# A two-layer trunk: seven, then eight column groups over the first k tiles in four phases, larger modulation loads, mixer A begun in the last phase

## The chip, the cores and the metric

The kernel runs on one core of a Trainium2 chip. The metric is the device time of one execution in microseconds (us). In this text PE is TensorE (matmuls), PEld its weight loads, DVE is VectorE, ACT is ScalarE, POOL is GpSimd, and SP is the engine whose queue issues most DMAs. Numbers such as L319 are lines of the kernel before; where a line of the changed kernel is meant, that is said.

## The reference

Two layers work on 384 tokens of width 2048, 128 of a context and 256 latents. What matters here is layer 0 and its order:

```python
sh, sc, gt = split(silu(cond) @ w_mod + b_mod, 3)          # w_mod [2048, 6144], two conditions
h = rmsnorm(x) * (1 + sc) + sh
aq, af_f, af_b, ai, ag, bq, bk, bv, bg = split(h @ w_in)   # w_in [2048, 7680]
o_a = hgrn2(silu(aq), gates(af_f), gates(af_b), ai)        # mixer A, 8 heads, both directions
o_b = attention(bq, bk, bv)                                # mixer B
y = x + gt * (concat(gated o_a, gated o_b) @ w_out)        # w_out [2048, 2048]
```

Layer 1 has a modulation, an input product, an attention and an output product of its own. Each product is made in three terms, high by high, high by low and low by high, of values that are split into a high and a low part.

## The kernel before, in words

**The products.** The k dimension of 2048 is 16 tiles of 128. A trunk product is made in column groups of 512 columns, a group in pieces of two k tiles: `w_piece` (L312) loads 512 KB of weights on SP's queue into one of four buffers `raw`, ACT writes the high part `whi` (L317, three buffers) and DVE the low part `wlo` (L319, two buffers). A piece is 24 matmuls of 384 columns, or 18 of 512 when the tokens are on the partitions. The sums of a group stand in four PSUM buffers `mm` (`psm`, L57), four or three to a group.

**The start.** Layer 0's input needs shift and scale of a k tile before that tile can enter a product. So the start goes through the k tiles in five phases, `START` = (0, 1), (1, 3), (3, 6), (6, 10), (10, 16). In each, `start_group` (L652) makes the partial product of six column groups (`first`: the forget gates `lf` and queries `qs` of mixer A) over the phase's k tiles and adds it to a tile in SBUF: a copy on ACT in the first phase, an addition on DVE (L670) later. Between the pieces `start_mod` (L672) loads the shift and scale weights of the next phase's k tiles, 512 KB at a time, into the same four buffers `raw`, and multiplies them on PE (L683, L691), after which `modulate` makes that part of the input.

**The background.** Everything else of the modulations is made on DVE, 1024 columns at a time, by `mod_acc` (L223): for each of 16 k tiles a load of 512 KB into one of two buffers `mraw`, and two additions to `acc` (L235), one for each condition. The list is, in order, layer 1's scale and shift (four parts), then the gates of layer 0, columns 0 to 1023 (`mod_gates`, L260, which ends with matmuls that spread `acc` over the partitions, L277 and L278, and additions to the tiles `tK` and `tL`, L279). After each piece of a product `pump` (L297) adds a rate to a counter and runs one unit (one k tile) of the list for each whole number in it. A step of a mixer takes a quarter of its own weight from that counter. `finish` (L303) runs units until a named gate is there.

**The order after the start.** Mixer A (`hgrn_prep`, `hgrn_heads`) is queued and takes a step after each piece of five groups: two for its values `vt`, two for the queries of mixer B, one for its keys and values. Then come four gate groups, with mixer B, and the output product. Its first group ends with `finish((0, 0))`, and its three sums are multiplied with the gate in `tK` (L991), which frees its PSUM buffers. The gates of columns 1024 to 2047 enter the list there. A scheduler places the instructions of each engine in one fixed order; an engine runs them in that order.

Of the kernel before, what the change touches and what calls it, by code (L numbers as in the profile page):

```python
# [14 lines left out]
P = 128  # L15
# [7 lines left out]
RATE0 = 0.6  # L23
# [7 lines left out]
SRAW = 3  # L31
# [5 lines left out]
START = ((0, 1), (1, 3), (3, 6), (6, 10), (10, 16))  # L37

# columns of the constant table
# [5 lines left out]
def trunk_kernel(ctx: ExitStack, tc: tile.TileContext, I, O):  # L45
# [8 lines left out]
    # what only the start needs  # L54
# [20 lines left out]
    # The mixers are traced step by step, one step after each piece of a trunk product, so that TensorE  # L75
    # has trunk products to run while a mixer's data is on its way through the other engines.
# [35 lines left out]
    # x, token-major: block 0 is the context, blocks 1 and 2 the latents  # L112
# [9 lines left out]
    # rows of parameters, turned into columns; the conditions first  # L122
# [17 lines left out]
    # silu of the two conditions, columns (k tile, condition)  # L140
# [18 lines left out]
    def load_params():  # L159
# [3 lines left out]
        # lower bound of the forget gates: softmax over the depth axis, first entry  # L163
# [38 lines left out]
    # ---------------------------------------------------------------- modulation  # L202
# [6 lines left out]
    def mod_cols(l, k0, nk, cp):  # L209
        # columns k0.. of the modulation, from sums [128, nk, 2] or [128, 2, 2, 2]  # L210
# [12 lines left out]
    def mod_acc(l, c0):  # L223
        # 1024 columns on VectorE, summed over the k tiles
# [15 lines left out]
    def mod_part(l, k0):  # L240
        # shift or scale of 8 k tiles, as columns
# [18 lines left out]
    def mod_gates(l, g0, tags, ready):  # L260
        # two times 512 columns of the gate as rows on all partitions, [128, 2, 512]
# [21 lines left out]
    # modulations in the background, pace[1] steps after each piece of a trunk product; gates that have  # L283
    # a place to go to come before the columns of layer 1
# [37 lines left out]
    def group(w, c0, hq, fm, after=None, n=512):  # L322
        # n columns of a product: 4 tiles [128 features, 384 tokens], or 3 tiles [128 tokens, n features]
# [33 lines left out]
    # ---------------------------------------------------------------- norm and modulation of x  # L357
# [5 lines left out]
    def turn_x(x, xt, copy):  # L363
        # [128 tokens, 512] x 3 -> [128 features, 4, 384]; copy(out, in, k tile of x)
# [6 lines left out]
    def rpow(out, ss, n, eps):  # L371
        # (ss / n + eps) ** -0.5
# [3 lines left out]
    def rstd_row(ss):  # L376
        # the norm's factors of all tokens, on all partitions
# [13 lines left out]
    def modulate(l, q, xt, rb, hq=None, parts=((0, 4),)):  # L391
        # x of a quarter, [128 features, 4, 384], normed, modulated in place and split
# [13 lines left out]
    def modulate_scaled(l, q, xt, rb, parts):  # L406
        # the same for x that the scale is in already
# [14 lines left out]
    def split(dst, k, src, scale=None):  # L422
        # dst = (high, low) tiles of a quarter, src [128, 384] in SBUF or PSUM, times a column
# [47 lines left out]
    def rope(x, nh, cw, sw):  # L471
        # in place on x [128, nh*128]
# [199 lines left out]
    def start_mod(k0, k1):  # L672
        # shift and scale of a few k tiles on TensorE, four k tiles of the product side by side
        for k, nk in pairs(k0, k1):
            n, k8 = nk * P, 8 // nk
            ps = px()
            for part in range(2):
                for i in range(2 * nk):
# [6 lines left out]
                    if part == 0 or i < 2 * nk - 1:  # L685
                        yield
# [21 lines left out]
    for i, (k0, k1) in enumerate(phases):  # L708
# [13 lines left out]
        if i == 1:  # L722
            load_params()
# [422 lines left out]
```

## Time and profile before

| | us |
|---|---|
| device time, three runs | 1397.18, 1395.74, 1390.61 |
| median | 1395.74 |
| span of the profiled execution, first to last instruction | 1388.5 |
| PE busy, share of the span | 1346.3, 97% |
| DVE busy | 1022.3, 74% |
| ACT busy | 651.8, 47% |
| DMA moved | 265.45 MB, mean 191 GB/s |

The profile gives the profiled execution's span; its time with what lies around the span is not listed by itself, and the median of the runs is 7.2 us above the span. A busy share of PE is an upper bound, since the end of a matmul is modelled. The page cuts the span in 40 slices; other views group instructions by line, list waits by who waited for whom, follow the chain of work that ended last, or give busy times of chosen stretches.

### The profile page before, as it was taken

The page shows a single profiled execution, that of the slowest core. Times are in us where ns is not written, and L with a number is a line of the kernel's source. Part 1 is how long each engine was busy: PE and PEld are TensorE (multiplying, and loading weights), DVE is VectorE, ACT ScalarE, POOL GpSimd, SP SyncE. Part 2 cuts the span into 40 slices and gives each one's busy share as a digit, 9 for nine tenths or more (in the row PEclk, how much of TensorE's full clock was granted, in tenths as well). Part 3 has the DMA queues.
Part 4 walks back from the last instruction along what each step waited for, and adds up shares of the span by engine and source line. Part 5 has one row for each costly group of instructions (what it writes and reads, how often), then busy time and mean ns, then how long its engine had stood idle before and what let it go on. Part 6 is the DMA issues. An engine that isn't in the chain of part 4 may idle for free.

```text
span 1388.5 us, 19820 instructions
## 1 busy us (share of the span) xinstructions
PE 1346.3 (97%) x7435; PEld 1152.5 (83%) x7435; DVE 1022.3 (74%) x1605; ACT 651.8 (47%) x1302; POOL 79.1 (6%) x86
## 2 busy tenths in 40 slices
PE   6999999999999999999998998999999999999998
PEld 5677888997888877788977896878888899997788
DVE  6587657998996989994896358985656664488753
ACT  4422333485654535655532345434866763352221
POOL 1000000000000032101000000100000001000000
PEclk9999999999999999999999998999999999999999
DMA  9999988647554576665477543774323345457742
GB/s 280 310 319 304 305 289 299 222 125 238 171 172 133 150 219 199 199 213 182 152 235 250 167 148 89 232 246 143 105 79 90 95 113 173 131 174 226 238 162 71
DMA packets 142239, 265.45 MB, mean 191 GB/s; under 512 B 8960, under 2 KB 54976, under 8 KB 142144
## 3 DMA queue, kind: packets, MB, share of 16 engines
q1 hardware_dynamic: 136288, 245.73, 56.2%
q0 software_dynamic: 5600, 18.39, 4.3%
q8 instruction: 58, 0.95, 0.3%
q14 instruction: 37, 0.30, 0.1%
q10 hardware_dynamic: 256, 0.08, 0.0%
HBM read 256.04 MB, written 8.13 MB: 190 GB/s over the span
## 4 chain that ended last, share of the span: by engine, by line
PE 82%; DVE 8%; DMA 5%; issue 2%; POOL 1%; ACT 1%; SPq 0%; DVEq 0%; POOLq 0%; ACTq 0%
PE mm L340 54%; PE mm L662 5%; PE mm L664 5%; PE mm L663 5%; DMA mraw<-in_l_w_mod_dram 4%; DVE acc L235 3%; PE px L520 3%; PE px L683 2%; DVE wlo L319 2%; PE px L580 1%; PE px L597 1%; POOL sm L374 1%; PE px L543 1%; PE px L368 1%; PE px L831 1%
## 5 line engine op out<-in xcount | busy, mean ns | idle before, releaser
L317 ACT CAST whi<-raw 128x1024 fp32r<-128x1024 f32 (+1 forms) x270 | 278.2, 1031 | 524.0 <-PE mm L340 392.4
L319 DVE TENSOR_TENSOR wlo<-raw,whi 128x1024 fp32r<-128x1024 f32 (+1 forms) x270 | 322.7, 1196 | 182.3 <-PE mm L340 155.0
L340 PE MATMUL mm<-wlo,hh 128*128 128x512 f32 (+1 forms) x1104 | 413.8, 375 | 13.3 <-DVE wlo L319 13.2
L340 PE MATMUL mm<-whi,hh 128*128 128x512 f32 (+1 forms) x1104 | 417.5, 378 | 1.2 <-ACT hh L417 0.8
L340 PE MATMUL mm<-whi,hl 128*128 128x512 f32 (+1 forms) x1104 | 411.7, 373 | 0.0
L235 DVE SCALAR_TENSOR_TENSOR acc<-mraw,csil,acc 128x1024 f32<-128x1024 f32 x240 | 300.9, 1278 | 37.2 <-DMA mraw<-in_l_w_mod_dram 36.9
L340 PEld LDWEIGHTS mm<-wlo,hh 128*128 128x128 f32 x1104 | 209.6, 190 | 53.3 <-DVE wlo L319 19.5
L340 PEld LDWEIGHTS mm<-whi,hh 128*128 128x128 f32 x1104 | 209.2, 190 | 39.2 <-issue 1.7
L340 PEld LDWEIGHTS mm<-whi,hl 128*128 128x128 f32 x1104 | 209.2, 190 | 35.9
L662 PE MATMUL mm<-hh,whi 128*128 128x384 f32 x384 | 134.1, 354 | 4.5 <-ACT whi L317 2.1
L340 PE MATMUL mm<-hh,whi 128*128 128x384 f32 x384 | 131.4, 342 | 0.8 <-DVE tM L613 0.8
L663 PE MATMUL mm<-hl,whi 128*128 128x384 f32 x384 | 130.6, 340 | 0.4 <-DVE hl L403 0.4
L340 PE MATMUL mm<-hh,wlo 128*128 128x384 f32 x384 | 129.4, 337 | 0.0
L340 PE MATMUL mm<-hl,whi 128*128 128x384 f32 x384 | 129.0, 336 | 0.0
L664 PE MATMUL mm<-hh,wlo 128*128 128x384 f32 x384 | 121.8, 340 | 0.1
L662 PEld LDWEIGHTS mm<-hh,whi 128*128 128x128 f32 x384 | 73.2, 192 | 21.1 <-issue 12.2
L664 PEld LDWEIGHTS mm<-hh,wlo 128*128 128x128 f32 x384 | 71.8, 189 | 4.1 <-DVE wlo L319 2.3
L663 PEld LDWEIGHTS mm<-hl,whi 128*128 128x128 f32 x384 | 73.3, 191 | 1.7 <-issue 1.0
L340 PEld LDWEIGHTS mm<-hh,whi 128*128 128x128 f32 x384 | 72.2, 188 | 2.8 <-DVE tM L613 1.6
L340 PEld LDWEIGHTS mm<-hl,whi 128*128 128x128 f32 x384 | 72.2, 188 | 0.9
L340 PEld LDWEIGHTS mm<-hh,wlo 128*128 128x128 f32 x384 | 72.1, 188 | 0.7 <-issue 0.2
L555 ACT ACTIVATE p<-px,nb,rs 128x384 f32<-128x384 f32 (+1 forms) x72 | 42.4, 594 | 12.2 <-DVE nb L553 8.2
(444 smaller groups left out, 1416.6 us busy)
## 6 DMA issues: line engine op xcount, KB each, us to landing
raw<-in_l_w_in_dram SPq DMA_DIRECT2D x194, 512.0 KB, 3.9
mraw<-in_l_w_mod_dram SPq DMA_DIRECT2D x192, 512.0 KB, 4.8
raw<-in_l_w_out_dram SPq DMA_DIRECT2D x64, 512.0 KB, 4.1
raw<-in_l_w_in_dram SPq DMA_DIRECT2D x12, 256.0 KB, 6.6
tK<-in_l_b_mod_dram POOLq DMA_DIRECT2D x6, 256.0 KB, 5.4
y1d<-tA POOLq DMA_DIRECT2D x2, 768.0 KB, 5.9
tD<-y1d POOLq DMA_DIRECT2D x2, 768.0 KB, 6.8
tL<-y1d POOLq DMA_DIRECT2D x2, 768.0 KB, 7.0
```

Of the source, the lines that this page charges most:

```text
L235: nc.vector.scalar_tensor_tensor(out=acc[:, c], in0=raw, scalar=s, in1=acc[:, c], op0=ALU.mult, op1=ALU.add)
L317: nc.scalar.copy(hi, raw)
L319: nc.vector.tensor_tensor(out=lo, in0=raw, in1=hi.bitcast(F32), op=ALU.subtract)
L340: nc.tensor.matmul(ps[c], lhsT=a, rhs=b, start=(kt + k == 0 and i == 0), stop=(kt + k == KT - 1 and i == 2))
L368: nc.tensor.transpose(ps[:, b * P:b * P + P], x[:, b, k * P:k * P + P], ident)
L374: nc.gpsimd.tensor_tensor(out=out, in0=out, in1=nhalf[:, 0:out.shape[1]], op=ALU.pow)
L520: nc.tensor.matmul(out, lhsT=a, rhs=b, start=(i == 0), stop=(i == len(ops) - 1))
L555: nc.scalar.activation(p[:, j], ss[j], AF.Exp, bias=nb[:, j:j + 1], scale=rs[:, i + j:i + j + 1], accum_out=sm[:, j:j + 1])
L662: nc.tensor.matmul(ps[c][:, 0:T], lhsT=wh, rhs=hh[:, kq], start=(kt + k == k0), stop=False)
L663: nc.tensor.matmul(ps[c][:, 0:T], lhsT=wh, rhs=hl[:, kq], start=False, stop=False)
L664: nc.tensor.matmul(ps[c][:, 0:T], lhsT=wl, rhs=hh[:, kq], start=False, stop=(kt + k == k1 - 1))
L683: nc.tensor.matmul(ps[32 * (j % 4):32 * (j % 4) + 32, part * n:part * n + n], lhsT=cs32[:, kt, :], rhs=raw[:, j], start=(kt < 4), stop=(kt ...
```

## The change

The start has four phases. Seven column groups take part from the first phase (the values `vt[0]` of mixer A join, with tokens on the partitions). In the third phase an eighth, `vt[1]`, makes up its first seven k tiles at once, and takes part in the fourth. The weights of shift and scale come in loads of 1 MB into two buffers of their own (`m8`), and the pieces of products use the four buffers `raw` alone. The background has a rate of its own in each phase: none in the first two, 0.2 in the third, 0.75 in the last. Mixer A's steps begin inside the last phase, after the third group. Some tiles have other tags, and the first constants come in two loads on two queues.

```diff
-RATE0 = 0.6
+RATE0 = (0.0, 0.0, 0.2, 0.75)
-SRAW = 3
+M8B = 2
-START = ((0, 1), (1, 3), (3, 6), (6, 10), (10, 16))
+START = ((0, 1), (1, 3), (3, 7), (7, 16))
...
-    nc.sync.dma_start(ct, I["consts"])
+    nc.sync.dma_start(ct[:, 0:C_SCAN], I["consts"][:, 0:C_SCAN])
+    nc.gpsimd.dma_start(ct[:, C_SCAN:C_ALL], I["consts"][:, C_SCAN:C_ALL])
...
-    first = [(lf[0][0], 1024), (lf[1][0], 2048), (lf[0][1], 1536), (lf[1][1], 2560), (qs[0], 0), (qs[1], 512)]
+    FM, TM = True, False
+    vt[0], vt[1] = tm_tile("M"), None
+    work = [(lf[0][0], 1024, FM), (lf[1][0], 2048, FM), (qs[0], 0, FM), (lf[0][1], 1536, FM), (lf[1][1], 2560, FM),
+            (qs[1], 512, FM), (vt[0], 3072, TM)]
...
-            hi, lo = w_piece(spool, "sraw", SRAW, W0, kt, n, c0, 512)
+            hi, lo = w_piece(wpool, "raw", RAWB, W0, kt, n, c0, 512)
...
-            n, k8 = nk * P, 8 // nk
+            n, k8 = nk * P, 16 // nk
...
-                for i in range(2 * nk):
-                    raw = wpool.tile([P, k8, n], F32, tag="raw", bufs=RAWB, name=nm("mraw"))
+                for i in range(nk):
+                    raw = spool.tile([P, k8, n], F32, tag="m8", bufs=M8B, name=nm("m8"))
...
-    pace[1] = RATE0
...
-    for i, (k0, k1) in enumerate(phases):
...
+    for i, (k0, k1) in enumerate(phases[:-1]):
+        pace[1] = RATE0[i]
+        k2, k3 = phases[i + 1]
+        nxt, n_nxt = start_mod(k2, k3), sum(2 * nk for _, nk in pairs(k2, k3))
+        items = [(*w, k0, k1, k0 == 0) for w in work]
+        if i == 2:
+            vt[1] = tm_tile("E")
+            items.append((vt[1], 3584, TM, 0, k1, True))
...
+    pace[1] = RATE0[-1]
+    k0, k1 = phases[-1]
+    items = [(*w, k0, k1, False) for w in [*work, (vt[1], 3584, TM)]]
+    begins = {2: lambda: hgrn_prep(0), 5: lambda: hgrn_prep(1), 6: lambda: hgrn_heads(0), 7: lambda: hgrn_heads(1)}
+    for j, it in enumerate(items):
+        for _ in start_group(*it):
+            step()
+            pump()
+        if j in begins:
+            queue.append(begins[j]())
     pace[1] = RATE
-    queue.append(hgrn_prep(0))
-    for g in range(2):
-        vt[g] = tm_tile("GH"[g])
-        evict_tm(group_b(W0, 3072 + 512 * g, h0), vt[g])
-        queue.append(hgrn_heads(g))
-        if g == 0:
-            queue.append(hgrn_prep(1))
```

**Order 1, DVE at the end of the first output group, before.** `wlo` is the low part of a weight piece (the first row's piece is the group's last), `acc` the background sum, here of the second pair of gates, `tA` the product of a sum in PSUM (`mm`) with the gate `tK`.

```order
L319 TENSOR_TENSOR wlo_6498<-raw_6494,whi_6496 128x1024
L235 SCALAR_TENSOR_TENSOR acc_6586<-mraw_6907,csil,acc_6586 128x1024 x2
L319 TENSOR_TENSOR wlo_6542<-raw_6538,whi_6540 128x1024
L235 SCALAR_TENSOR_TENSOR acc_6586<-mraw_6959,csil,acc_6586 128x1024
L991 TENSOR_TENSOR tA_6518<-mm_6323,tK_6062 128x512
```

**Order 2, the same place in the changed kernel.** Here `acc` is the sum of the first pair of gates, `alo` its low part, and `tK` the gate that the group's own sums wait for. On DVE, ten additions to `acc` and three rows that end the gate now stand between the low part of the group's last piece and the first `tA`, where three additions stood.

```order
L320 TENSOR_TENSOR wlo_6445<-raw_6441,whi_6443 128x1024
L236 SCALAR_TENSOR_TENSOR acc_6092<-mraw_6469,csil,acc_6092 128x1024 x2
L320 TENSOR_TENSOR wlo_6551<-raw_6547,whi_6549 128x1024
L236 SCALAR_TENSOR_TENSOR acc_6092<-mraw_6473,csil,acc_6092 128x1024 x2
L320 TENSOR_TENSOR wlo_6604<-raw_6600,whi_6602 128x1024
L236 SCALAR_TENSOR_TENSOR acc_6092<-mraw_6477,csil,acc_6092 128x1024 x2
L236 SCALAR_TENSOR_TENSOR acc_6092<-mraw_6481,csil,acc_6092 128x1024 x2
L236 SCALAR_TENSOR_TENSOR acc_6092<-mraw_6485,csil,acc_6092 128x1024 x2
L277 TENSOR_TENSOR alo_6495<-acc_6092,ahi_6493 128x512
L280 TENSOR_TENSOR tK_6489<-px_6492,tK_6489 128x512
L277 TENSOR_TENSOR alo_6503<-acc_6092,ahi_6501 128x512
L1007 TENSOR_TENSOR tA_6527<-mm_6242,tK_6489 128x512
```

**Order 3, PE behind it, in the changed kernel.** The last row of the first output group, then the second group's first sum (`mm_1165`, one PSUM buffer was free: twelve matmuls of two pieces, of which the first and the last stand here), one of a third piece, the gate's spreading matmuls, and the second group's second sum.

```order
L341 MATMUL mm_1108_6244<-whi_1138_6443,hl3_1100_6222 128x512
L341 MATMUL mm_1165_6544<-whi_1169_6549,hh0_1056_5937 128x512
...
L341 MATMUL mm_1165_6544<-whi_1178_6602,hl0_1057_5938 128x512
L341 MATMUL mm_1165_6544<-whi_1182_6630,hh1_1071_6036 128x512
L278 MATMUL px_1147_6492<-ahi_1148_6493,ones_r_82 128x512
L279 MATMUL px_1147_6492<-alo_1149_6495,ones_r_82 128x512
L278 MATMUL px_1150_6500<-ahi_1151_6501,ones_r_82 128x512
L279 MATMUL px_1150_6500<-alo_1152_6503,ones_r_82 128x512
L278 MATMUL px_1154_6511<-ahi_1155_6512,ones_r_82 128x512
L341 MATMUL mm_1166_6545<-whi_1169_6549,hh0_1056_5937 128x512
```

Behind the thirteen matmuls PE has the gate's own matmuls next, in a fixed order; before, the gate's matmuls stood two groups earlier.

**Order 4, DVE at the end of the last phase, in the changed kernel.** `tE` is `vt[1]`, whose three sums are added from PSUM (L680 there); `attz`, `att`, `hg`, `dt`, `dd` belong to mixer A.

```order
L320 TENSOR_TENSOR wlo_3300<-raw_3296,whi_3298 128x1024
L848 COPY_PREDICATED attz_1904<-mk,px_3186 128x384
L848 COPY_PREDICATED attz_1905<-mk,px_3196 128x384
L792 SCALAR_TENSOR_TENSOR hg_3212<-ct,tA_267 128x384
L853 TENSOR_TENSOR att_3206<-attz_1904,attz_1905 128x384
L800 TENSOR_TENSOR tA_267<-hg_3212 128x384
L833 TENSOR_TENSOR dt_3231<-dd_3217 128x1
L794 SCALAR_TENSOR_TENSOR hg_3268<-ct,tC_269 128x384
L680 TENSOR_TENSOR tE_999<-tE_999,mm_3051 128x512
```

The addition that frees a PSUM buffer stands behind mixer A's rows; before, the groups beside mixer A were copied out by ACT (L727).

## Rows read from the trace of the kernel before

**Rows 1.** The page, busy time of two engines, share of the span and instructions

```profile
PE 1346.3 (97%) x7435; PEld 1152.5 (83%) x7435; DVE 1022.3 (74%) x1605; ACT 651.8 (47%) x1302; POOL 79.1 (6%) x86
```

**Rows 2.** Stretches: start:end length, busy us of each engine, granted clock, DMA

```profile
core 0: us, PE busy (x) PEld busy (x) DVE busy (x) ACT busy (x) POOL busy (x), PEclk, DMA share, GB/s
...
28.00:300.00 272.00, 264.51 (x1748) 224.66 (x1749) 204.34 (x275) 110.17 (x160) 2.03 (x3) 0.98 0.85 281
300.00:510.00 210.00, 209.51 (x1139) 175.59 (x1138) 187.29 (x331) 116.79 (x232) 17.72 (x21) 1.00 0.58 174
510.00:705.00 195.00, 192.50 (x957) 161.10 (x958) 163.87 (x234) 103.49 (x229) 21.68 (x19) 1.00 0.63 193
705.00:768.00 63.00, 58.21 (x256) 46.61 (x255) 47.89 (x47) 21.54 (x36) 5.10 (x8) 0.97 0.73 240
```

**Rows 3.** Who PE waited for, 28 to 100 us: total, times, longest

```profile
PE mm L662 <- ACT hh L402: 1.3, 2, 0.9
PE px L683 <- DMA mraw<-in_l_w_mod_dram: 1.0, 1, 1.0
PE px L691 <- ACT ev L688: 0.7, 1, 0.7
PE mm L662 <- ACT whi L317: 0.6, 1, 0.6
PE mm L663 <- DVE hl L403: 0.4, 1, 0.4
```

**Rows 4.** The same, 100 to 300 us, the two longest

```profile
PE mm L662 <- ACT whi L317: 1.5, 2, 1.1
PE mm L662 <- DVE tB L670: 0.8, 1, 0.8
```

**Rows 5.** Stretches within the start, columns as in rows 2

```profile
28.00:100.00 72.00, 67.58 (x469) 51.34 (x470) 49.27 (x77) 30.42 (x56) 0.59 (x1) 0.96 0.96 317
100.00:300.00 200.00, 196.93 (x1281) 173.31 (x1280) 155.07 (x199) 79.75 (x104) 1.44 (x2) 0.99 0.81 268
```

**Rows 6.** The chain in order of time: one piece of a product (start, us, what)

```profile
616.64 4.17 PE mm L340 x24
...
374.28 4.12 PE mm L340 x18
```

**Rows 7.** PE groups of 28 to 300 us: busy us, mean ns, idle before

```profile
L683 PE MATMUL px<-mraw,cs 128*32 128x256 f32 (+1 forms) x504 | 39.5, 376 | 1.0 <-DMA mraw<-in_l_w_mod_dram 1.0
L691 PE MATMUL px<-ct,ev 128*128 128x2 f32 x60 | 7.8, 250 | 1.4 <-ACT ev L688 1.4
```

**Rows 8.** DVE groups of 705 to 768 us: busy us, mean ns, idle before

```profile
L235 DVE SCALAR_TENSOR_TENSOR acc<-mraw,csil,acc 128x1024 f32<-128x1024 f32 x20 | 25.0, 1280 | 9.3 <-DMA mraw<-in_l_w_mod_dram 9.3
L319 DVE TENSOR_TENSOR wlo<-raw,whi 128x1024 fp32r<-128x1024 f32 x14 | 17.1, 1219 | 4.6 <-PE mm L340 2.9 <-issue 1.7
L991 DVE TENSOR_TENSOR tA<-mm,tK 128x512 f32<-128x512 f32 x3 | 2.0, 681 | 0.0
```

**Rows 9.** DVE in order of time: the first gate's last rows, then its first use

```profile
665.18 0.68 DVE L279 TENSOR_TENSOR tK<-px,tK 128x512 f32<-128x512 f32 x1
...
671.40 0.68 DVE L279 TENSOR_TENSOR tL<-px,tL 128x512 f32<-128x512 f32 x1
...
722.23 1.28 DVE L991 TENSOR_TENSOR tA<-mm,tK 128x512 f32<-128x512 f32 x2
```

**Rows 10.** Who PE waited for, 700 to 770 us

```profile
PE mm L340 <- DVE wlo L319: 4.1, 3, 3.2
```

**Rows 11.** Stretches of 4 us around a stall of PE, columns as in rows 2

```profile
852.00:856.00 4.00, 1.11 (x6) 0.61 (x4) 4.00 (x10) 3.20 (x8) 0.00 (x0) 0.98 0.00 0
856.00:860.00 4.00, 4.00 (x11) 3.20 (x12) 4.00 (x10) 1.68 (x5) 0.00 (x0) 0.59 0.47 131
```

**Rows 12.** One line, its durations min/median/max in ns, first and last start

```profile
L670 DVE TENSOR_TENSOR tL<-tL,mm x16: 520/550/555, 87.4 to 298.7; 128x384 f32<-128x384 f32 x16
```

More of the change, by code (lines that the diff above doesn't have):

```diff
@@ L650, in pairs, with start_group @@
         return out
-    def start_group(acc, c0, k0, k1, copy):
-        ps = [psm.tile([P, 512], F32, tag="mm", name=nm("mm")) for _ in range(4)]
+    def start_group(acc, c0, fm, k0, k1, copy):
+        nt, w = (4, T) if fm else (3, 512)
+        ps = [psm.tile([P, 512], F32, tag="mm", name=nm("mm"))[:, 0:w] for _ in range(nt)]
         for kt, n in pairs(k0, k1):
-            hi, lo = w_piece(spool, "sraw", SRAW, W0, kt, n, c0, 512)
+            hi, lo = w_piece(wpool, "raw", RAWB, W0, kt, n, c0, 512)
@@ L657, in start_group @@
             hh, hl = h0[kt // 4]
-            for c in range(4):
+            for c in range(nt):
+                cs = slice(c * P, c * P + P)
                 for k in range(n):
                     kq = kt % 4 + k
-                    wh, wl = hi[:, k, c * P:c * P + P], lo[:, k, c * P:c * P + P]
-                    nc.tensor.matmul(ps[c][:, 0:T], lhsT=wh, rhs=hh[:, kq], start=(kt + k == k0), stop=False)
-                    nc.tensor.matmul(ps[c][:, 0:T], lhsT=wh, rhs=hl[:, kq], start=False, stop=False)
-                    nc.tensor.matmul(ps[c][:, 0:T], lhsT=wl, rhs=hh[:, kq], start=False, stop=(kt + k == k1 - 1))
+                    if fm:
+                        ops = ((hi[:, k, cs], hh[:, kq]), (hi[:, k, cs], hl[:, kq]), (lo[:, k, cs], hh[:, kq]))
+                    else:
+                        ops = ((hh[:, kq, cs], hi[:, k]), (hh[:, kq, cs], lo[:, k]), (hl[:, kq, cs], hi[:, k]))
+                    for i, (a, b) in enumerate(ops):
+                        nc.tensor.matmul(ps[c], lhsT=a, rhs=b, start=(kt + k == k0 and i == 0),
+                                         stop=(kt + k == k1 - 1 and i == 2))
@@ L665, in start_group @@
             yield
-        for c in range(4):
+        for c in range(nt):
             if copy:
-                nc.scalar.copy(acc[:, c], ps[c][:, 0:T])
+                nc.scalar.copy(acc[:, c], ps[c])
             else:
-                nc.vector.tensor_tensor(out=acc[:, c], in0=acc[:, c], in1=ps[c][:, 0:T], op=ALU.add)
+                nc.vector.tensor_tensor(out=acc[:, c], in0=acc[:, c], in1=ps[c], op=ALU.add)
     def start_mod(k0, k1):
         for k, nk in pairs(k0, k1):
-            n, k8 = nk * P, 8 // nk
+            n, k8 = nk * P, 16 // nk
@@ L684, in start_mod @@
                                          lhsT=cs32[:, kt, :], rhs=raw[:, j], start=(kt < 4), stop=(kt >= KT - 4))
-                    if part == 0 or i < 2 * nk - 1:
+                    if part == 0 or i < nk - 1:
                         yield
@@ L696, in start_mod @@
             yield
-    def start_products(k0, k1):
-        for acc, c0 in first:
-            yield from start_group(acc, c0, k0, k1, k0 == 0)
     phases = START
@@ L704, in trunk_kernel @@
     mods += [mod_part(1, k0) for k0 in (16, 24, 0, 8)] + [mod_gates(0, 0, "KL", ready0)]
-    pace[1] = RATE0
     for _ in start_mod(*phases[0]):
         pass
-    for i, (k0, k1) in enumerate(phases):
-        nxt, n_nxt = iter(()), 0
-        if i + 1 < len(phases):
-            k2, k3 = phases[i + 1]
-            nxt, n_nxt = start_mod(k2, k3), 4 * (k3 - k2)
-        n = len(first) * len(pairs(k0, k1))
-        done = 0
-        for j, _ in enumerate(start_products(k0, k1)):
-            while done < (j + 1) * n_nxt // n:
-                next(nxt, None)
-                done += 1
-            pump()
+    for i, (k0, k1) in enumerate(phases[:-1]):
[6 more added lines that the diff above has]
+            items.append((vt[1], 3584, TM, 0, k1, True))
+        n = sum(len(pairs(it[3], it[4])) for it in items)
+        done = j = 0
+        for it in items:
+            for _ in start_group(*it):
+                j += 1
+                while done < j * n_nxt // n:
+                    next(nxt, None)
+                    done += 1
+                pump()
         for _ in nxt:
```

12 lines of the change are left out of this document (7 added, 5 removed).

## The prediction

> **What bounds the kernel now.** I read the page first: PE is busy for 97% of the span [rows 1], DVE for 74%. That says only that PE is the engine to look at, so next come the stretches [rows 2]. Four of them cover what the change touches: the start (28 to 300 us), mixer A (300 to 510), the gate groups (510 to 705) and the first output groups (705 to 768). PE is without work for 272 - 264.5 = 7.5 us in the first, 0.5 in the second, 2.5 in the third and 4.8 in the fourth. The change takes no matmul away: the same column groups go over the same 16 k tiles, so what it can give back is PE's waiting and a clock below full speed, and what it can cost is new waiting. The third view is who PE waited for in the start [rows 3, 4]: single waits of about 1 us, 4.0 us listed up to 100 us and 2.3 in the two longest after. The fourth is DVE beside it. In the mixer's stretch DVE is busy for 187 of 210 us and PE still hardly waits; in the first output groups DVE itself waits 9.3 us for loads of background weights [rows 8], and PE then 4.1 us for DVE [rows 10]. So the reader should see a kernel with little left to win on PE, and two places where DVE is close to setting the pace.
>
> **The change part by part.**
>
> *The start.* Before, 36 pieces precede the last phase, and at 0.6 units a piece they bring 21 units of 512 KB, 11 MB; the change brings 25 x 0.2 = 5 units there. DMA moved 317 GB/s from 28 to 100 us with its engines 96% busy [rows 5], so 16 units fewer are about 8.4 MB / 317 GB/s = 26 us of transfers. But PE only had 7.5 us of waiting, and a mean clock of 0.98 (272 x 0.02 = 5.4 us of lost speed). Of the waits, those for `hh`, `ev` and `hl` (1.3 + 0.7 + 0.4) belong to the chain at the end of a phase, which stays: the last modulation, its copy, its columns, the input's parts. What can go is the wait for a load, for `whi` and for the additions (1.0 + 0.6 + 1.5 + 0.8 = 3.9 us), and about 1 us of clock. I take **-5 us**.
>
> The bounds of this term. A piece of 24 matmuls takes 4.17 us on PE and one of 18 takes 4.12 [rows 6]. The start before has 6 groups x 16 tiles x 12 matmuls = 1152 at 4.17 / 24 = 0.174 us, 200 us; with the modulations' 39.5 and 7.8 [rows 7] and about 6 us of others that is 253 of 272 us. So no more than 19 us can come back. The other way, the third phase now loads nine k tiles of shift and scale (nine of 2.1 MB), 28 k tiles of weights of 262 KB and seven of `vt[1]`, and 5 units, 30.6 MB: 97 us at 317 GB/s. PE's work there is 28 x 2.09 + 7 x 2.06 + 9 x (39.5 + 7.8) x 16 / (14 x 16) = 58 + 14 + 30 = 103 us, so DMA is close behind PE and a late load can cost a little: I bound it by +5.
>
> The loads of 1 MB carry the same bytes in half as many. *DMA: Bandwidth & Descriptors* (the Trainium skill, Measured, under Bandwidth) says that loads should be batched to 1 MB or more to get three quarters of the peak, and gives 341 GB/s for one of 1 MB. No row here has such a load; by that rule the larger loads would push the start towards its bound of -19. The rows of this trace show the engines 96% busy already with 512 KB in flight fourfold, so I leave the term at -5.
>
> The first constants come in two loads: PE's first wait is not for them, so this is nothing; were it the first x that comes earlier, under 1 us.
>
> *Mixer A in the last phase.* Its matmuls are the same and run beside products before and after. Since PE waited 0.5 us in that stretch, nothing is to be had. What is new is that sums which ACT copied out now are added by DVE, in DVE's order behind mixer A's rows (order 4). An addition is 0.55 us [rows 12], a background unit 2 x 1.28 [rows 8]; the next group needs the same four PSUM buffers. In the last phase before, PE waited 0.8 us for such additions [rows 4]. There are eight boundaries of groups; if one unit stood before each, less what PE still has to do, that is 0 to 10 us. DVE ran up to two pieces ahead of PE in most of it, so I take **+3**.
>
> *The gates come late.* This is the largest term. Up to mixer B the background before has 32 units in the start (54 pieces x 0.6) and 52 in five groups (40 x 1.3), less the mixer's share; the change has 5 + 30 (40 x 0.75) + 31 (24 x 1.3), less the same share: 18 units fewer. Before, the gate of the first columns was finished at 665 to 671 us and first used at 722 [rows 9], 50 us of slack. Afterwards it is not finished in time: order 2 shows ten additions and the gate's ending between the low part of the first output group's last piece and the first `tA`, which frees PSUM for the second group. On DVE that is 10 x 1.28 + 2 x 1.22 + 3 x 0.68 + 0.68 = 18.0 us. (The 0.68 is that of the gate's rows [rows 9].) PE has in that time the last piece, 4.1 us, and thirteen matmuls of the next group (order 3), 13 x 4.12 / 18 = 3.0; if DVE is two whole pieces ahead, another 4.1. So PE stands for at least 18.0 - 11.2 = 6.8 us. At most, the loads are late as they are now: 9.3 us for 20 additions, here 4.7 for ten, and DVE is not ahead, 18.0 + 4.7 - 7.1 = 15.6 us. PE was waiting for `wlo` in the group before [rows 10], so DVE is not ahead, and I take **+13**, near the upper end.
>
> After PE had stood, the granted clock was 0.59 over the next 4 us, most of it at the lower of its two levels, 1.2 GHz [rows 11]: **+2** more, 0 to 2. With the first gate late, the second pair's additions move from the first two output groups to the second and third. The third then has 17 of them, 21.8 us, beside 9.8 of low parts and 4.1 of sums, 35.7 against PE's 8 x 4.12 = 33: **+3**, 0 to 8.
>
> What nothing is counted for: fewer additions of partial sums (three phases instead of four, seven or eight groups), which DVE makes in the start where it is idle for a quarter of the time [rows 2]; were that cover gone, they are under 0.6 us each.
>
> **The sum** is -5 + 3 + 13 + 2 + 3 = +16 us. It is made against the profiled execution, span 1388.5; the median of the runs is 1395.7, and moved by 16 us it is **1412 us**, 1.1% slower.
>
> **The rivals.**
>
> *The start gives all it has* (faster). DMA at 96% is what held PE below its own pace from 28 to 300 us, and with 8.4 MB less in front of it all 19 us come back, while the gate costs its floor of 6.8, and the other two nothing: -12 us, 1384. For it speaks the DMA share, against it that the waits listed are small and half belong to the chain at a phase's end. It decides if the start gains more than the gate costs: over 14 us against 7 is needed to leave the band of no change.
>
> *The late gate is mostly covered* (no change). DVE, relieved of 16 units early, arrives two pieces ahead at the end of the first output group, and the loads are there: -5 + 6.8 + 0 to 3, between 1396 and 1401. For it speaks that DVE waited for PE in the third stretch; against it, that the same background now fills the group before.
>
> *DVE falls behind in the last phase* (much slower). Its two rates together ask for more than PE's time: three groups with mixer A's rows and 0.75 units a piece. Then each boundary costs a unit and the tail of mixer A is late: +10 in place of +3, and the gate at its upper end, 15.6 + 2 + 8: with -5 about +31, 1426.
>
> **How the numbers follow.** Half a percent, 7 us, is about what a measurement of this kernel can tell from no change. My forecast has 0.53, the last rival 0.15, no change 0.22 and the first rival 0.10. Slower is then 0.68, same 0.22, faster 0.10. The range leaves out the first rival and half of the last one: the low end is a start that gives its waiting and clock (-13) with the gate's floor, 1390; the high end stands just above the last rival, 1430.
>
> **What would show it.** In the profile of the changed kernel: the start up to the end of the last phase shows PE waiting 2 to 5 us between 28 and 180 us; DMA over its first 70 us is below 317 GB/s or no longer at 96%. At the end of the first output group, near 730 us, the timeline shows PE without work for 10 to 16 us, the wait named as the gate's `ahi`, `alo` or `tA`, and a clock near 0.5 right after. If no such hole stands there, the prediction is wrong in its largest term; if the start is shorter by over 10 us, in its first.

## The result and the profile after

The changed kernel takes 1405.9 us (median of 4 runs, 1404.9 to 1412.5) against 1396.1 before, a ratio of 1.0093 with a 95% interval of 1.0069 to 1.0117: 0.9% slower. The prediction was 1412 us, slower. The profiled execution took 1405.15 us and its span is 1403.3 us, 14.8 above the span before; the sum had said 16. The rows below are read on that execution.

First the stretches of [rows 2], the same four, and the first of [rows 5], in the changed kernel (the columns are those of rows 2).

```profile
28.00:300.00 272.00, 266.42 (x1846) 232.75 (x1847) 179.76 (x249) 116.53 (x178) 2.03 (x3) 0.98 0.82 265
300.00:510.00 210.00, 208.00 (x1141) 176.88 (x1140) 187.47 (x352) 116.33 (x249) 23.16 (x23) 1.00 0.53 165
510.00:705.00 195.00, 193.60 (x974) 162.18 (x973) 161.43 (x213) 98.08 (x202) 13.86 (x16) 1.00 0.65 200
705.00:768.00 63.00, 46.31 (x187) 34.62 (x186) 49.11 (x50) 17.42 (x28) 3.14 (x5) 0.92 0.67 213
...
28.00:100.00 72.00, 69.02 (x538) 56.84 (x539) 41.17 (x68) 32.68 (x61) 0.60 (x1) 0.93 0.93 292
```

Three stretches look much as before. In the fourth PE is without work for 16.7 of 63 us, 4.8 before, and its mean clock is 0.92. Next, the timeline of PE over 700 to 770 us, only the rows before which PE stood (start, duration, instruction; in brackets the idle time and what ended it).

```profile
706.44 0.50 PE L341 MATMUL mm<-wlo,hh 128*128 128x512 f32 x1 [0.68 <-DVE wlo L320]
713.95 0.50 PE L341 MATMUL mm<-wlo,hh 128*128 128x512 f32 x1 [1.76 <-DVE wlo L320]
723.07 0.80 PE L278 MATMUL px<-ahi,ones_r 128*128 128x512 f32 x1 [7.45 <-ACT ahi L275]
724.21 0.79 PE L279 MATMUL px<-alo,ones_r 128*128 128x512 f32 x1 [0.35 <-DVE alo L277]
726.39 0.80 PE L279 MATMUL px<-alo,ones_r 128*128 128x512 f32 x1 [0.68 <-DVE alo L277]
752.42 0.50 PE L341 MATMUL mm<-wlo,hh 128*128 128x512 f32 x1 [3.51 <-DVE wlo L320]
757.29 0.50 PE L341 MATMUL mm<-wlo,hh 128*128 128x512 f32 x1 [0.49 <-DVE wlo L320]
761.83 0.50 PE L341 MATMUL mm<-wlo,hh 128*128 128x512 f32 x1 [0.16 <-DVE wlo L320]
767.81 0.50 PE L341 MATMUL mm<-wlo,hh 128*128 128x512 f32 x1 [1.61 <-DVE wlo L320]
```

The first five are the hole at the end of the first output group, 10.9 us, and it is the gate's high part `ahi` that ends it. What DVE did in that time stands in its own timeline:

```profile
705.17 1.22 DVE L320 TENSOR_TENSOR wlo<-raw,whi 128x1024 fp32r<-128x1024 f32 x1
706.76 2.48 DVE L236 SCALAR_TENSOR_TENSOR acc<-mraw,csil,acc 128x1024 f32<-128x1024 f32 x2 [0.37 <-DMA mraw<-in_l_w_mod_dram]
709.15 1.22 DVE L320 TENSOR_TENSOR wlo<-raw,whi 128x1024 fp32r<-128x1024 f32 x1
710.29 2.48 DVE L236 SCALAR_TENSOR_TENSOR acc<-mraw,csil,acc 128x1024 f32<-128x1024 f32 x2
712.68 1.22 DVE L320 TENSOR_TENSOR wlo<-raw,whi 128x1024 fp32r<-128x1024 f32 x1
713.84 2.48 DVE L236 SCALAR_TENSOR_TENSOR acc<-mraw,csil,acc 128x1024 f32<-128x1024 f32 x2
717.07 2.48 DVE L236 SCALAR_TENSOR_TENSOR acc<-mraw,csil,acc 128x1024 f32<-128x1024 f32 x2 [0.74 <-DMA mraw<-in_l_w_mod_dram]
721.08 2.48 DVE L236 SCALAR_TENSOR_TENSOR acc<-mraw,csil,acc 128x1024 f32<-128x1024 f32 x2 [1.53 <-DMA mraw<-in_l_w_mod_dram]
723.48 0.68 DVE L277 TENSOR_TENSOR alo<-acc,ahi 128x512 fp32r<-128x512 f32 x1
...
726.25 0.68 DVE L1007 TENSOR_TENSOR tA<-mm,tK 128x512 f32<-128x512 f32 x1
```

These are the ten additions and two low parts of order 2. From the end of the first row's low part (706.4) to the end of the first `tA` they take 20.5 us where the prediction had 18.0; 2.6 of them are loads that were late. The clock behind the hole, in stretches of 4 us and one of 8 (before, its stall: [rows 11]), falls to the lower level, 1.2 GHz:

```profile
720.00:724.00 4.00, 0.80 (x1) 0.29 (x1) 2.92 (x3) 0.62 (x1) 0.00 (x0) 0.51 0.50 142
724.00:728.00 4.00, 3.11 (x5) 1.68 (x6) 2.83 (x6) 1.24 (x2) 0.00 (x0) 0.50 0.42 131
728.00:732.00 4.00, 4.00 (x14) 3.11 (x14) 3.00 (x5) 0.62 (x1) 1.06 (x2) 0.71 0.08 23
732.00:740.00 8.00, 8.00 (x43) 6.64 (x42) 7.67 (x10) 6.14 (x16) 2.08 (x3) 1.00 0.74 203
```

To see where the 14.8 us came from, both kernels (and six of the experiments) are set side by side at the same points of the program, the ends of the last copy, sum or product that empties a group's PSUM, in us from the span's start:

| point | before | changed | e1 | e2 | e5 | e6 | e8 | e12 |
|---|---|---|---|---|---|---|---|---|
| `kv0` copied out | 510.1 | 499.2 | 501.2 | 504.2 | 520.7 | 498.2 | 496.8 | 513.0 |
| last gate group | 692.1 | 679.0 | 688.4 | 685.9 | 702.3 | 678.6 | 673.1 | 700.0 |
| output group 1 | 725.8 | 729.7 | 721.0 | 739.9 | 736.0 | 721.0 | 706.7 | 732.6 |
| output group 3 | 802.7 | 815.5 | 804.3 | 827.1 | 813.2 | 792.9 | 777.1 | 806.0 |
| output group 5 | 838.1 | 850.9 | 839.6 | 862.5 | 848.5 | 828.3 | 815.2 | 841.4 |
| span | 1388.5 | 1403.3 | 1389.8 | 1416.4 | 1401.3 | 1373.1 | 1359.8 | 1385.4 |

The changed kernel is 10.9 us ahead when `kv0` is copied out and 13.1 at the last gate group. It loses 17.0 in the first output group, 8.9 in the next two, and 2.0 from there to the end.

### The profile page after: what moved, and what is told of

It is laid out like the page before. It is cut to its first block, busy times and chain, and to the rows that moved or that the text cites. A ratio compares the mean times of both kernels' runs of the same rounds, so it can differ in the third digit from the quotient of the medians.

```text
span 1403.3 us, 19971 instructions
## 1 busy us (share of the span) xinstructions
PE 1343.7 (96%) x7499; PEld 1155.4 (82%) x7499; DVE 1022.6 (73%) x1607; ACT 652.3 (46%) x1313; POOL 73.3 (5%) x87
## 4 chain that ended last, share of the span: by engine, by line
PE 62%; DVE 8%; DMA 6%; issue 2%; ACT 0%; POOL 0%; DVEq 0%; POOLq 0%
PE mm L341 49%; DMA mraw<-in_l_w_mod_dram 5%; DVE acc L236 4%; PE mm L673 3%; PE px L521 2%; DVE wlo L320 2%; PE px L581 1%; PE px L598 1%; PE px L544 1%; PE px L844 1%; DMA raw<-in_l_w_out_dram 1%; PE px L847 0%; PE px L861 0%; PE px L511 0%; PE px L535 0%
## 5 line engine op out<-in xcount | busy, mean ns | idle before, releaser
L341 PE MATMUL mm<-wlo,hh 128*128 128x512 f32 (+1 forms) x1008 | 377.8, 375 | 19.1 <-DVE wlo L320 19.1
L341 PE MATMUL mm<-whi,hh 128*128 128x512 f32 (+1 forms) x1008 | 380.4, 378 | 1.4 <-ACT hh L418 0.8
L341 PE MATMUL mm<-whi,hl 128*128 128x512 f32 (+1 forms) x1008 | 375.8, 373 | 0.0
L236 DVE SCALAR_TENSOR_TENSOR acc<-mraw,csil,acc 128x1024 f32<-128x1024 f32 x240 | 301.5, 1281 | 46.0 <-DMA mraw<-in_l_w_mod_dram 45.6
L341 PEld LDWEIGHTS mm<-wlo,hh 128*128 128x128 f32 x1008 | 191.9, 190 | 57.6 <-DVE wlo L320 27.0
L341 PEld LDWEIGHTS mm<-whi,hh 128*128 128x128 f32 x1008 | 191.6, 190 | 35.1 <-issue 1.7
L341 PEld LDWEIGHTS mm<-whi,hl 128*128 128x128 f32 x1008 | 191.7, 190 | 32.1
L341 PE MATMUL mm<-hh,wlo 128*128 128x384 f32 x384 | 129.4, 337 | 0.0
L673 PE MATMUL mm<-hh,wlo 128*128 128x384 f32 x384 | 128.7, 337 | 0.0
```

The source lines that it names most:

```text
L236: nc.vector.scalar_tensor_tensor(out=acc[:, c], in0=raw, scalar=s, in1=acc[:, c], op0=ALU.mult, op1=ALU.add)
L341: nc.tensor.matmul(ps[c], lhsT=a, rhs=b, start=(kt + k == 0 and i == 0), stop=(kt + k == KT - 1 and i == 2))
L673: nc.tensor.matmul(ps[c], lhsT=a, rhs=b, start=(kt + k == k0 and i == 0), stop=(kt + k == k1 - 1 and i == 2))
```

## The experiments

The theory: the first gate comes late, DVE makes its additions one after the other, and PE stands until they are done. The rivals: the start's new form costs the time; DVE is full anyway, so that the wait only moves; and, later, the loads of the background are the cost rather than its additions. The kernel before was measured again beside each set of runs, with medians of 1393.7 to 1396.1 us; the ratios are to that, and times of different sets can differ by 2 us for it alone.

**e1: no unit left for the end of the first output group.** On the changed kernel:

```diff
-RATE = 1.3
+RATE = 1.5
```

> The changed kernel with 1.5 background units a piece after the last phase instead of 1.3, so that no unit is left to be made at the end of the first output group. Theory (the late gate is the cost): the hole of PE near 723 us goes (7.5 us for ahi and the waits around it, 10.9 us in that group), the clock stays at 1.00, and the second pair's additions come a group earlier as before the change (7 us); the ten units more are 10 x 2.56 = 25.6 us of DVE in groups where it is idle for a tenth to a quarter of the time. 1385 to 1391 us, below both kernels. Rival (DVE is full, the wait only moves): PE waits as much for wlo between 366 and 640 us, 1402 to 1408 us. Second rival (the start's own form costs the time): 1400 to 1406 us.

Measured: 1392.3 us, ratio to before 0.9995 (0.9979 to 1.0011). The hole is gone: PE is busy for all 32.6 us of the first output group at clock 1.00. In the table the first output group ends 8.7 us earlier than in the changed kernel, though the group before it ends 9.4 later: 18 us were won by work that runs beside mixer B instead, and half of them paid there. The time is a little above the range: of the 7 us that the second pair was to give back little came, output groups 2 and 3 take 83.3 us, 85.8 in the changed kernel and 76.9 before.

**e2: the late gate alone.** On the kernel before:

```diff
-RATE0 = 0.6
+RATE0 = 0.25
```

> The kernel before with 0.25 units a piece in the start instead of 0.6, so that seven units are left to be made at the end of the first output group, as in the changed kernel; its phases, loads and mixer A as they were. Theory (the late gate is the cost): PE idle for 8 to 12 us near 730 us with the clock lower behind it, 13 to 15 us in all, and 3 to 7 us more in the two groups behind; the start gives back at most 5 us. 1406 to 1415 us. Rival (the changed start is what costs the time, the hole only replaces another wait): 1392 to 1398 us.

Measured: 1422.7 us, ratio 1.0209 (1.0187 to 1.0231). The hole stands in the old kernel too, with the same name (who PE waited for, 20 to 860 us: total, times, longest; then the stretch of the first output group):

```profile
PE px L277 <- ACT ahi L274: 10.2, 2, 8.9
...
686.00:740.00 54.00, 40.74 (x157) 31.10 (x156) 46.23 (x46) 11.96 (x15) 0.00 (x0) 0.86 0.65 206
```

That stretch has 13.3 us without work and a clock of 0.86. So the mechanism needs nothing of the changed phases. It is larger than expected: 20.3 us in the first output group, 10.3 in the next two, and the start gives back 5.9 by `kv0`. Together with e1 this settles the place; the size was still not understood.

**e4: the size of the start's loads.** On the changed kernel, 512 KB in four buffers (the loops and counts follow):

```diff
-M8B = 2
+M8B = 4
-            n, k8 = nk * P, 16 // nk
+            n, k8 = nk * P, 8 // nk
-                for i in range(nk):
+                for i in range(2 * nk):
```

> The changed kernel with the start's modulation loads of 512 KB in four buffers instead of 1 MB in two. Theory (the start's loads are not what sets the time): within 3 us of the changed kernel, 1403 to 1409 us, with DMA over 28 to 100 us back above 300 GB/s (292 in the changed kernel). Rival (two buffers of 1 MB let the DMA run dry in the first phases and cost PE its waits for m, 2.4 us listed, and the clock of 0.93): 1396 to 1402 us. Second rival (large loads are the gain of the start): 1409 to 1416 us.

Measured: 1408.7 us, ratio 1.0107 (1.0088 to 1.0126): the changed kernel's own, within the intervals. DMA over 28 to 100 us did not come back over 300 GB/s, it moved 281. That part of the theory was wrong, and so was the rival: the size and number of the loads, with the same 2 MB of buffers, are not what lowers it. *DMA: Bandwidth & Descriptors* (the Trainium skill, Measured, under Bandwidth) wants loads of 1 MB or more; in this kernel 292 GB/s with them and 281 with half of it made no difference in time that could be measured.

**e5: the later modulations don't wait.** On the changed kernel:

```diff
-RATE0 = (0.0, 0.0, 0.2, 0.75)
+RATE0 = (0.6, 0.6, 0.6, 0.75)
```

> The changed kernel with 0.6 units a piece in the first three phases, as before the change, instead of 0, 0 and 0.2 (last phase unchanged): the later modulations no longer wait, and the unit counts from the first output group on are those of the kernel before. Theory: the hole goes as with the higher rate after the start, and the start pays the background's loads back with up to 5 us: 1387 to 1396 us, 0 to 5 us above the run with the higher rate. Rival (the background in the start is free, as PE waits there for the chain at a phase's end): equal to the run with the higher rate within 2 us. Second rival (the changed phases themselves cost): 1400 to 1406 us.

Measured: 1402.8 us, ratio 1.0074 (1.0060 to 1.0089). The hole is gone here as well (33.7 us in the first output group, as before the change), but the kernel is 21.5 us behind the changed one at `kv0`. Ten of its units more fall into the third phase. That phase in the changed kernel, then in e5, with who PE waited for in e5:

```profile
96.00:196.00 100.00, 99.51 (x773) 80.02 (x772) 53.69 (x91) 34.15 (x55) 0.00 (x0) 1.00 0.95 313
```

```profile
99.00:217.00 118.00, 106.85 (x757) 83.09 (x757) 74.67 (x112) 34.87 (x57) 0.00 (x0) 0.97 0.90 302
...
PE mm L673 <- ACT whi L318: 8.0, 5, 3.7
PE mm L673 <- DVE wlo L320: 2.6, 3, 1.4
```

In the changed kernel PE and DMA are both full in the third phase, 99.5% and 95%. Ten loads of 0.52 MB more at 302 GB/s are 17 us, and the phase is 18 us longer. So the new phases need it that the later modulations wait, and at a rate of 1.3 behind the start the late gate is what that costs. The theory's 5 us was far too little, since it took the start's idle time for room on the DMA.

**e3: mixer A not begun in the start.** On the changed kernel, all four parts are queued behind the last group:

```diff
-        if j in begins:
-            queue.append(begins[j]())
+        if j == 7:
+            queue.extend(f() for f in begins.values())
```

> The changed kernel with all four parts of mixer A queued behind the start's last group instead of inside it; the seven late units stay. Theory (the early begin costs little in the start, at most the sums' waits of about 2 us, and spares the drain behind the last projection): six steps of the mixer are left for that drain, where PE has no product beside them, so 10 to 30 us slower than the changed kernel: 1415 to 1435 us. Rival (mixer A's early begin is one of the costs, +3 in the sum): 1400 to 1405 us.

Measured: 1420.8 us, ratio 1.0188 (1.0169 to 1.0208), as the theory had it. Within the new phases the early begin is not a cost but worth 13 us by the ratios, 15 by the times. At the points of the table e3 is 9.2 us ahead of the changed kernel when `kv0` is copied out (490.0) and 16.7 behind at the last gate group (695.7): the mixer's steps have moved behind `kv0`, where the drain runs them without a product beside them.

**e6: a third buffer for the background's loads.** On the changed kernel:

```diff
-MRAWB = 2
+MRAWB = 3
```

> The changed kernel with three buffers for the background's loads instead of two; units and orders as in the changed kernel. Theory (of the hole, 2.6 us between the last low part and the first tA are loads that came late: 0.37 + 0.74 + 1.53; the rest are additions): 1402 to 1405 us, the hole still there, 5 to 7 us. Rival (the loads are late because the DMA is full there, a third buffer changes nothing): 1405 to 1409 us. Second rival (the loads are the whole of the hole, DVE's additions would fit beside PE): 1390 to 1397 us.

Measured: 1374.9 us, ratio 0.9859 (0.9843 to 0.9874): 31 us less than the changed kernel, and none of the three expectations. The additions' group on the pages of the changed kernel and of e6 (count, busy, mean ns, idle before them and its releaser):

```profile
L236 DVE SCALAR_TENSOR_TENSOR acc<-mraw,csil,acc 128x1024 f32<-128x1024 f32 x240 | 301.5, 1281 | 46.0 <-DMA mraw<-in_l_w_mod_dram 45.6
...
mraw<-in_l_w_mod_dram SPq DMA_DIRECT2D x128, 512.0 KB, 4.5
```

```profile
L236 DVE SCALAR_TENSOR_TENSOR acc<-mraw,csil,acc 128x1024 f32<-128x1024 f32 x240 | 298.7, 1282 | 4.5 <-DMA mraw<-in_l_w_mod_dram 4.5
```

The additions are the same, but DVE stands 45.6 us for their loads with two buffers and 4.5 with three. A load takes 4.5 us from issue to landing (last column), and a buffer is free again only after two additions, 2.5 us; two buffers thus bring two units in 7 us, 3.5 us each, where DVE alone needs 2.5. While DVE stands for a load, the low part behind it in its order stands too. I had counted the 2.6 us of late loads that lie in the hole itself. In the table e6 wins 8.3 us in the first output group, 13.9 more up to the end of the third and 7.6 behind the fifth. In output groups 2 and 3 PE stands for 0.5 us, 12.0 in the changed kernel. DVE's wait for these loads from 640 to 830 us, in the changed kernel and in e6:

```profile
DVE acc L236 <- DMA mraw<-in_l_w_mod_dram: 21.6, 15, 6.6
```

```profile
DVE acc L236 <- DMA mraw<-in_l_w_mod_dram: 2.1, 2, 1.4
```

In the hole of the changed kernel the last three pairs of additions begin 3.2 and 4.0 us apart, which is this pace. What is left of the hole in e6 is 5.0 us, most of it in one row:

```profile
714.45 0.51 PE L278 MATMUL px<-ahi,ones_r 128*128 128x512 f32 x1 [3.78 <-ACT ahi L275]
```

**e11: the same loads on another queue.** On the changed kernel with its two buffers:

```diff
-            nc.sync.dma_start(raw, I[f"l{l}_w_mod"]
+            nc.gpsimd.dma_start(raw, I[f"l{l}_w_mod"]
```

> The changed kernel with two buffers, its background's loads issued on POOL's queue instead of SP's. It tells apart why a third buffer helped. Theory (latency: a load can be issued only when its buffer is free and lands 4.6 us later, so two buffers give a unit every 3.5 us where DVE needs 2.5, whichever queue issues it): 1400 to 1410 us, DVE's wait for these loads 40 us or more. Rival (order on SP's queue: the issue stands behind a product's load that waits for wlo, and the products' loads behind it): 1372 to 1390 us, the wait down to 15 us or less.

Measured: 1422.7 us, ratio 1.0204 (1.0183 to 1.0224). DVE waits more, not less, and each load lands as late as before:

```profile
L236 DVE SCALAR_TENSOR_TENSOR acc<-mraw,csil,acc 128x1024 f32<-128x1024 f32 x240 | 301.3, 1280 | 62.0 <-DMA mraw<-in_l_w_mod_dram 61.8
...
mraw<-in_l_w_mod_dram POOLq DMA_DIRECT2D x128, 512.0 KB, 4.7
```

This speaks against the order on SP's queue as the cause. The issues of the changed kernel itself, SP's in the hole, settle it:

```profile
709.26 0.33 SPq L230 DMA_DIRECT2D mraw<-in_l_w_mod_dram  x1
710.40 0.38 SPq L316 DMA_DIRECT2D raw<-in_l_w_out_dram  x1
712.79 0.33 SPq L230 DMA_DIRECT2D mraw<-in_l_w_mod_dram  x1
713.93 0.38 SPq L316 DMA_DIRECT2D raw<-in_l_w_out_dram  x1
716.35 7.56 SPq L230 DMA_DIRECT2D mraw<-in_l_w_mod_dram  x3
```

The additions that free the buffers end at 709.24, 712.77 and 716.32 us in DVE's timeline above, and each load is issued 0.02 to 0.03 us later; so are all 32 loads between 640 and 830 us. Nothing on the queue holds them; what is left is the time from issue to landing over two buffers, which the pace above fits. On POOL's queue the issue comes 0.30 us after the buffer is free, which fits DVE's longer wait. Of the 17 us that e11 is slower than the changed kernel (15 by the ratios), 12 are there when `kv0` is copied out (511.1): up to there PE waits 10.5 us for the start's loads `m`, 2.4 in the changed kernel. Why those loads come later was not followed further. *Trainium Kernel Development and Optimization* (the Trainium skill, Key Constraints) says that several issuing queues share the same DMA engines and save only issue time; this run, with no gain from a second queue, agrees. Its Best Practices ask for double buffers; here two were not enough, and the run with three decides.

**e9: the third buffer in the kernel before.**

```diff
-MRAWB = 2
+MRAWB = 3
```

> The kernel before with three buffers for the background's loads instead of two, nothing else. Theory (two buffers hold DVE up in both kernels, and the late gate makes the changed one pay more for it): DVE waits 36.9 us for such loads before, 45.6 after, and before has no hole at the first output group; it gains 8 to 18 us, 1377 to 1387 us, so that with three buffers the change is worth 2 to 12 us (1374.9 in the changed kernel with three). Rival (before has its additions off the path): 1390 to 1396 us, the change is worth 20 us with three buffers. Second rival (before gains as much or more): 1360 to 1374 us, the change costs with three buffers as well.

Measured: 1387.3 us, ratio 0.9936 (0.9921 to 0.9952), 0.3 us above the theory's range. With three buffers in both kernels the change turns from 0.9% slower to 0.8% faster (0.9859 / 0.9936 = 0.992). DVE's wait for these loads falls to 7.7 us here too, but the kernel is 12.6 us behind the kernel before at `kv0` (522.7), and wins that and 2 us more behind it. Part of the loss is in mixer A, where PE now stands for the mixer's rows (who PE waited for, 337 to 433 us):

```profile
PE px L831 <- DVE hg L798: 3.3, 1, 3.3
PE px L868 <- DVE s L855: 0.8, 1, 0.8
```

In the kernel before, the same stretch (332.7 to 420.3) had no wait at all. It is 8.4 us longer in e9: PE stood 4.8 us in it, and the mean clock was 0.96 where it had been 1.00, 3.8 us of lost speed. Why the third buffer costs here and not in the changed kernel (498.2 at `kv0` against 499.2) stays open.

**e7, e8 and e10: both mends together.** e7 is e1 with `MRAWB = 3`; e8 has 1.1 for `RATE1` in addition, so that no unit is left at the end of the third output group. e10 was to have a fourth buffer in addition, but the kernel that ran has `MRAWB = 3`: it is e8's kernel once more, and its expectation stays untested.

```diff
-RATE = 1.3
+RATE = 1.5
-RATE1 = 0.9
+RATE1 = 1.1
-MRAWB = 2
+MRAWB = 3
```

> The run with 1.5 units a piece, with three buffers for the background's loads too. Theory: what that run still loses against the kernel before lies in the second and third output groups (83.3 us for both, 76.9 before), where DVE waits 12.3 us for such loads and PE 6.3 us for wlo; a third buffer takes a third to two thirds of it: 1387 to 1391 us. Rival (DMA sets these groups: 76% busy, 247 GB/s): 1391 to 1394 us. Second rival (a load further ahead holds the products' own loads up on SP's queue): 1394 to 1400 us.

> As the run before, and 1.1 instead of 0.9 units a piece from the last gate group on, so that the end of the third output group has no unit left to be made (three before). Theory: these three, 3 x 2.56 = 7.7 us of DVE with the gate's rows behind them, hold the third group's tA by 2 to 5 us as the seven did in the first; spread over 24 pieces they hide: 1384 to 1390 us. Rival (DVE has no room in the first two output groups either): 1390 to 1396 us.

> The fastest run so far (1.5 and 1.1 units a piece, three buffers) with a fourth buffer. Theory (with three, DVE waits for these loads 4 to 5 us in all, so that DVE's additions and PE are what is left): within 3 us, 1359 to 1365 us. Rival (latency still shows in the groups with forced units): 1352 to 1358 us.

Measured: e7 1366.0 us (ratio 0.9793, 0.9777 to 0.9809), e8 1362.4 (0.9770, 0.9755 to 0.9785), and e10, the same kernel again, 1364.0 (0.9780, 0.9766 to 0.9794). e7 is 21 us below its range, for the reason found in e6. From e7 to e8 come 3.6 us, to its repeat 2.0: the size expected for the three late units, but the intervals overlap, so this gain is not shown. Whether a fourth buffer would help is not shown either; DVE's wait for these loads is down to 3.1 us in e8 and 6.8 in its repeat. e8 is 2.3% faster than the kernel before (2.2% in its repeat) and the fastest of the study.

**e12: everything of e8 but the change's form of the start.** On the kernel before: `MRAWB = 3`, `RATE0 = 0.25`, `RATE = 1.5`, `RATE1 = 1.1`.

> The kernel before (five phases of six groups, mixer A behind the start) with three buffers for the background's loads and a background that leaves no unit for the end of an output group: 0.25 units a piece in the start, 1.5 behind it, 1.1 from the last gate group on. It has everything of the fastest run but the change's own form of the start. Theory (with the gates in time, the change's phases and mixer A begun inside the start are a gain of the size that the milestones gave, 5 to 13 us): 1367 to 1376 us, against 1362.4 for the fastest run. Rival (the form of the start is worth nothing, buffers and rates do it all): 1360 to 1365 us. Second rival (mixer A and 1.5 units a piece do not fit in DVE before): 1377 to 1387 us.

Measured: 1384.8 us, ratio 0.9921 (0.9897 to 0.9944), the second rival's range. Against e8, at these rates, the new phases and mixer A's early begin are worth 22 us (21 by the ratios): by the table 16.2 at `kv0`, 10.7 more up to the last gate group, and nothing behind it. How much of the 16.2 is what the third buffer cost e9 there is open, and no other rates were tried on the kernel before.

## Why the prediction was right, term by term

**The late gate, +13, and the clock, +2: right in mechanism, place and sum.** The first output group, before and in the changed kernel (columns of [rows 2]):

```profile
692.10:725.80 33.70, 33.43 (x146) 26.94 (x145) 30.51 (x32) 9.67 (x11) 0.00 (x0) 1.00 0.69 225
```

```profile
679.00:729.70 50.70, 39.78 (x159) 30.56 (x158) 43.80 (x45) 11.94 (x15) 0.00 (x0) 0.91 0.65 208
```

PE stood 10.9 us, 0.3 before: 10.6 where 13 were forecast. The clock of 0.91 over 50.7 us would be 4.6 us, but the first 3 us of the lower level, from 720 us, lie in the standstill, where they slow nothing. PE's 6.0 busy us behind it, up to 730, cost half of that: an estimate of 3.0 us, above the term's range of 0 to 2. Together that is 13.6 where 15 were forecast, so each term is off a little and the other way. The rest of the 17.0 us are five of the gate's own matmuls, which before lay in the last gate group, and a few of the next group's. The wait had the name that was given, the place too (723 us), and e2 makes it alone in the old kernel. DVE was not ahead of PE, as forecast (PE waits 0.68 and 1.76 us for `wlo` in the hole), but the row this was read from fits it less well: of the 4.1 us of [rows 10] only 0.3 fall into the first output group.

**The second pair, +3 (0 to 8): mis-sized.** Output groups 2 and 3 lost 8.9 us, just above its upper end. The step that failed is that the term set DVE's work alone, 35.7 us, against PE's 33 and had no wait for loads. Per addition the loads were no later than the prediction had read (21.6 us for 60 additions between 640 and 830 us in the changed kernel, 9.3 for 20 before), but it had put them only into the upper bound of the first hole. Once DVE is not ahead of PE, each such wait goes through the next low part to PE. With three buffers, in e6, DVE stood 2.1 us for the same additions and PE 0.5 us in these two groups, against 12.0.

**The start, -5 (-19 to +5), and mixer A, +3 (0 to 10): together too small, and by another way than was said.** Up to `kv0` the two brought -10.9 us where the sum had -2. Some 2 us of that are a modulation part's matmuls that had not been made yet. The prediction looked for the gain in PE's waits and its clock, since the change takes no matmul away. The stretch up to `kv0` before, in the changed kernel and in e2:

```profile
0.00:510.10 510.10, 490.12 (x3018) 412.96 (x3018) 409.64 (x653) 239.36 (x423) 23.43 (x34) 0.99 0.74 236
```

```profile
0.00:499.20 499.20, 480.16 (x3068) 414.12 (x3069) 373.46 (x625) 239.99 (x433) 23.67 (x35) 0.99 0.71 224
```

```profile
0.00:504.20 504.20, 481.95 (x3002) 412.57 (x3002) 371.47 (x620) 242.72 (x424) 24.08 (x34) 0.98 0.70 221
```

PE stood 20.0 us before and 19.0 in the changed kernel, and the clock is the same; what fell is PE's busy time, by 10.0 us. The step that failed here is to read the 97% as work that stays: a busy share is an upper bound, and the views don't tell what the busy time held. In e2, where 19 units fewer in the old start are all that changed, it fell by 8.2 us, and e2 is 5.9 us ahead at `kv0` (2 of them the same modulation part): so taking loads out is worth about the 5 forecast. The other 5 us belong to the new phases and mixer A together, where the sum had +3. The waits for sums that the +3 stood for are 2.3 us up to the end of the start, and e3 shows the early begin to be worth 13 to 15 us within the new phases. No run parts the phases from the mixer in the old form. Put back, the removed loads cost 21.5 us in e5: in the new phases there is no room for them.

**The two errors went against each other.** Up to the last gate group the changed kernel was 13.1 us ahead where the sum had 2; from there on it lost 17.0 + 8.9 + 2.0 = 27.9 where the sum had 18 (some 2 us in both are the gate's matmuls, which moved across). 27.9 less 13.1 is 14.8, and 18 less 2 is 16: that the total came within 1.2 us, with parts that are 10 to 11 us off, is luck.

**The rivals.** *The start gives all it has* fell: the start gave 9 to 11 of its 19 us, and the gate with its clock cost 13.6 and not 6.8. *The late gate is mostly covered* fell with the hole. *DVE falls behind in the last phase* fell with 2.3 us of waits for sums (1.1 + 0.5 + 0.5 + 0.2) in the whole start. The views named beforehand: between 28 and 180 us PE is busy for 148.5 of 152 us, so it stood 3.5 us, within the 2 to 5 given. The waits listed there sum to 5.9, but the first of them ended at 28.2 us and lies almost wholly ahead of the stretch:

```profile
PE mm L673 <- ACT hh L403: 2.6, 1, 2.6
PE px L693 <- DMA m<-in_l_w_mod_dram: 2.4, 2, 1.9
PE px L701 <- ACT ev L698: 0.9, 1, 0.9
```

DMA fell to 292 GB/s and 93% over 28 to 100 us, and the clock after the hole was 0.50. The sign of being wrong in the first term, a start shorter by over 10 us, was nearly given: at the end of `vt[1]`, the last group of the changed start, the changed kernel is 8.9 us ahead (365.8 against 374.7), and 10.9 at `kv0`.

## What to carry to other kernels

When work is moved later, look for what must be finished at a fixed point behind it, and count the units that are left there. Price a unit not by the engine that does it but by the slower of the engine and its loads, which is the time from issue to landing, plus use, over the number of buffers. And before a restructuring is judged, give both versions the buffers and rates that suit them: as it stood, this change cost 0.9%; with a third buffer and rates that leave no unit, it is worth 22 us (e8 against e12).

## What the runs showed that was not expected

- A third buffer of 512 KB took DVE's wait for the background's loads from 45.6 to 4.5 us and the kernel from 1405.9 to 1374.9 us.
- The same loads on POOL's queue landed in 4.7 us, 4.5 on SP's, were issued 0.30 us after their buffer was free instead of 0.03, and made the kernel 17 us slower.
- Fewer loads in the start (e2) lowered PE's busy time up to `kv0` by 8.2 us, with no fewer trunk matmuls and no less waiting.
- In the start 28 to 100 us showed 281 to 304 GB/s with loads of 512 KB or 1 MB, with and without the background beside them (317 in the kernel before, [rows 5]).
